# A two-layer hybrid decoder trunk: narrower gate maxima, paired transposes and another TensorE planner

## The chip, the cores and the metric

The kernel runs on one core of a Trainium2 chip. A core has several engines that work side by side, each through its own queue in order: TensorE (matmuls and transposes, called PE in the profile), VectorE (DVE), ScalarE (ACT), GpSimd (POOL) and SyncE (SP, which issues the DMAs here). The metric is the time of one execution in device microseconds, as the median of several runs. The profile's span runs from the first to the last instruction and is a little shorter than that time.

## The reference, cut to what matters

Two layers, sequence 256, model width 1024. Each layer normalises x, multiplies it by one wide input matrix, feeds three groups of heads, joins their outputs and adds the output projection to x. A last RMSNorm ends it.

```python
def hybrid_layer(x, norm_w, w_in, conv_w, conv_b, gate_bias, ret_norm_w, mlstm_norm_w, w_out):
    h = rmsnorm(x, norm_w)
    proj = jnp.matmul(h, w_in).astype(jnp.float32)
    (aq, ak, av, ag, bq, bk, bv, bg, cq, ck, cv, co, cg, ci, cf) = jnp.split(proj, cuts, axis=-1)
    # group A, 8 heads x 64: causal softmax attention with ALiBi, SiLU gate ag
    ya = merge_heads(moba_attention(...)) * jax.nn.silu(ag)
    # group B, 4 heads x 64: retention with fixed decays, head norm, SiLU gate bg
    yb = head_norm(retention(...), ret_norm_w) * jax.nn.silu(bg)
    # group C, 4 heads x 64: mLSTM on convolved q, k; gates i, f; output gate co; head norm; SiLU gate cg
    yc = head_norm(mlstm(...) * jax.nn.sigmoid(co), mlstm_norm_w) * jax.nn.silu(cg)
    y = jnp.concatenate([ya, yb, yc], axis=-1)
    return x + jnp.matmul(y, w_out)
```

With a sequence of 256 group A has one block, so it is plain causal attention. In group C each position's weights are exp of (a gate term of the key minus a running maximum of the gate terms up to the query). That running maximum, per head, is the "gate maxima" of the change:

```python
        d_log = jnp.where(causal, bt[..., :, None] - bt[..., None, :] + it[..., None, :], -jnp.inf)
        m_t = jnp.maximum(inter_log, jnp.max(d_log, axis=-1))
        w_intra = jnp.exp(d_log - m_t[..., None])
```

## The kernel before

All of x stays on the chip, transposed (features on partitions). Every fp32 operand of a projection is split into a high part in the rounded fp32r format and the rest (`hi`, `lo` for weights, `xx` for x, `yh`, `yl` for the gated outputs); ScalarE makes the high part, VectorE subtracts (`splitter`, `split_x`). A product is three TensorE matmuls, hi*hi, hi*lo and lo*hi, or one matmul of 512 columns for the first two and one of 256. Weights stream from HBM in chunks of about 1 MB into three buffers (`raw`).

The order of the work is not written by hand. Each piece of work is a Python generator (a "thread") that yields one operation at a time with an engine and an assumed cost in nanoseconds. `Sched.run` replays the threads in planned time. Each time it issues the operation that can start first on its engine; among equals the smaller priority number wins, then age. A result made on one engine counts as ready for another after `LAT` = 230 ns. What comes out is a fixed order of instructions for each engine; on the chip, semaphores make each instruction wait for its inputs, and each engine takes its instructions strictly in this order.

- `project` (priority 5) is the TensorE thread of the projections. It is almost always ready and fills what others leave.
- Small threads turn a projection's result into heads. Four PSUM banks `pj` hold projection results, four banks `mx` everything else.
- `head_a` does one head of group A: four score matmuls (`dots`) into an `mx` bank, VectorE's add of the ALiBi distances with a row maximum (`tensor_tensor_reduce`, "CUSTOM_DVE_ANT_0 sb<-mx,tb" in the profile), two exponentials on ScalarE into `sb`, three TensorE transposes of `sb` (128x128 each) into another `mx` bank, a ScalarE copy to `et`. `pair_a` starts two heads, waits for both, and multiplies with the values.
- Before its transposes `head_a` waits 400 ns of planned time more, by a `pause`; `norm` waits 500 ns between GpSimd's power (-0.5) and two transposes. These are the only two pauses.
- In group C, `evac_cv` computes the running maxima of 4 heads in `cu`, [4, 256], and copies columns 128 to 256 again behind them, so `cu` has 384. `ub` holds their high and low parts. `head_c` spreads one head's row to all 128 partitions by a matmul with a selecting matrix `sel` (384 columns, "mx<-ub,sel"); VectorE adds the causal mask, 384 columns of a table: keys 0 to 127 against all 256 queries, then keys 128 to 255 against queries 128 to 255.
- `y_out` transposes gated outputs for the output projection; `last_in`, `last_add`, `last_norm`, `last_out` are the end of the kernel.

The assumed TensorE costs stand in `M` and `TR`. Lines 259, 265, 280, 285, 288 and 494 or 1101 of the profile are the helpers that issue VectorE, ScalarE, matmul, transpose, DMA and GpSimd operations.

Of the kernel before, what the change touches and what calls it, by code (L numbers as in the profile page):

```python
# [110 lines left out]
class Sched:  # L111
# [2 lines left out]


    LAT = 230.0
    SELF = {"pe": 0.0, "dve": 130.0, "act": 130.0, "pool": 130.0, "sp": 0.0}

    def __init__(self):
# [68 lines left out]
    def run(self):  # L188
        while self.live:
            best = None  # L190
            for th in self.live:
                alt = None
                for way in th.req[1:]:
                    eng, cost, fn, after = way
                    if after is not None:
                        ready = after
                    elif th.src is None:
                        ready = th.t
                    else:
                        ready = th.t + (self.SELF[eng] if th.src == eng else self.LAT)  # L200
                    if after is None:
                        ready = max(ready, th.floor)
                    start = max(self.free.get(eng, 0.0), ready)
                    if alt is None or start + cost < alt[0]:
                        alt = (start + cost, start, way)
                prio = th.prio() if callable(th.prio) else th.prio
                key = (alt[1], prio, th.seq)
                if best is None or key < best[0]:
                    best = (key, th, alt[2])
            (start, _, _), th, (eng, cost, fn, after) = best  # L210
            self.live.remove(th)
            ins = fn()
            if self.log is not None:
                self.log.append((eng, start, start + cost, ins.ins.name))
            end = start + cost
            self.free[eng] = end
            th.t, th.src = end, eng
            self.step(th, end + self.LAT)

# [9 lines left out]
def trunk(ctx: ExitStack, tc: tile.TileContext, xp: bass.AP, w: bass.AP, fn: bass.AP,  # L229
# [7 lines left out]
    def sb_tile(shape, name, dt=F32):  # L237
        return cp.tile(shape, dt, name=name)
# [35 lines left out]
    def M(out, a, b, start, stop, after=None):  # L274
        n = _n(b)
        if a.dtype == F32R:
            cost = max(107.0, n / 2.4) + 3
        else:
            cost = 2 * max(107.0, n * 2 / 2.4 / 1.0) + 3
        return op("pe", cost, lambda: nc.tensor.matmul(out, a, b, start=start, stop=stop, skip_group_check=True),  # L280
                  after)

# [7 lines left out]
    def wait(ev):  # L290
        return ("wait", ev)
# [4 lines left out]
    def acq(tag):  # L296
        return ("acq", tag)

    def pause(t):

        ev = Event()
        ev.time = t
        return wait(ev)


    px = sb_tile([128, P_N + KT * S], "px")
    pr = px[:, :P_N]
# [12 lines left out]
    yh = sb_tile([128, KT, S], "yh", F32R)  # L320
    yl = sb_tile([128, KT, S], "yl", F32R)
    sel = sb_tile([128, 4, 128], "sel", F32R)
    ub = sb_tile([128, 384], "ub", F32R)
    cu = sb_tile([4, 384], "cu")
    gi = sb_tile([4, 2, S], "gi")
    on_a = sb_tile([128, 2, 512], "on_a")
    on_b = sb_tile([128, 2, 256], "on_b")
# [145 lines left out]
    def norm(l):  # L473

        ss = None
        for k in range(0, KT, 2):
            for z in (k, k + 1):
                yield wait(E("x0", z) if l == 0 else E("res", l - 1, z))
            sq = yield acq("t512")
            yield A(sq, x[:, k:k + 2, :].rearrange("p a t -> p (a t)"), AF.Square)  # L480
            if ss is None:
                ss = sq
            else:
                e = yield V("tensor_tensor", ss, ss, sq, op=OP.add)
                sc.release("t512", sq, e)
        yield V("tensor_tensor", ss[:, :256], ss[:, :256], ss[:, 256:], op=OP.add)
        p = yield acq("mx")
        for b in range(2):
            e = yield M(p[:, b:b + 1], ss[:, b * 128:(b + 1) * 128], ones[:, 0:1], b == 0, True)
        sc.release("t512", ss, e)  # L490
        ms = tiny(2)
        yield V("tensor_scalar", ms, p[:, 0:2], 1.0 / D_, EPS, op0=OP.mult, op1=OP.add)
        rs = tiny(2)
        e = yield G(630, lambda: nc.gpsimd.tensor_tensor(rs, ms, mhalf[:, :2], op=OP.pow))
        yield wait(E("tab"))
        yield pause(e + 500)
        for b in range(2):
            yield TR(p[:, 128 + b * 128:256 + b * 128], rs[:, b:b + 1].to_broadcast([128, 128]))
        rh = tiny(2)
        yield V("tensor_scalar", rh, rs, 0.5, None, op0=OP.mult)  # L500
        e = yield A(rrow, p[:, 128:384], AF.Copy)
        sc.release("mx", p, e)
        norms[l] = (rs, rh)
        sc.set(E("rs", l), e)
        yield prio(2)
        yield V("tensor_tensor", cr, tb[:, T_COS:T_COS + S], rrow, op=OP.mult)
        e = yield V("tensor_tensor", sr, tb[:, T_SIN:T_SIN + S], rrow, op=OP.mult)
        sc.set(E("cs", l), e)
# [318 lines left out]
    def pair_a(l, g, u, box):  # L827
        rs, rh = norms[l]
        et = yield acq("et")
        done = [Event(), Event()]  # L830
        for hh in range(2):
            sc.spawn(head_a(l, g, u, hh, et, done[hh]), 2)
        yield wait(done[0])
        yield wait(done[1])
        box[0] += 1
        if box[0] == 2:
            drop(l, (f"aq{g}", f"ak{g}"), done[1].time)
        yield wait(E("va", l))
        po = yield acq("mx")
        pv = po[:, :260].rearrange("p (b h e) -> p b h e", b=2, h=2)  # L840
        for hh in range(2):
            h = 4 * g + 2 * u + hh
            yield M(pv[:, 0, hh, :], et[:, hh, 0:128], va[:, 0, h, :], True, True)
            yield M(pv[:, 1, hh, :], et[:, hh, 128:256], va[:, 0, h, :], True, False)
            e = yield M(pv[:, 1, hh, :], et[:, hh, 256:384], va[:, 1, h, :], False, True)
        sc.release("et", et, e)
        rv = tiny(2, 2)
        yield V("reciprocal", rv, pv[:, :, :, HD])
        yield V("tensor_tensor", rv, rv, rh.unsqueeze(2).to_broadcast([128, 2, 2]), op=OP.mult)
        c0 = (4 * g + 2 * u) * HD  # L850
        e = yield V("tensor_tensor", on_a[:, :, c0:c0 + 128].rearrange("p b (h e) -> p b h e", e=HD),
                    pv[:, :, :, 0:HD], rv.unsqueeze(3).to_broadcast([128, 2, 2, HD]), op=OP.mult)
        sc.release("mx", po, e)
        sc.set(E("ona", l, 2 * g + u), e)

    def head_a(l, g, u, hh, et, done):
        h = 4 * g + 2 * u + hh
        s_ = yield acq("mx")
        yield from dots(s_, bufs[l, f"aq{g}"], bufs[l, f"ak{g}"], u, hh, QK_CUTS)
        sb = yield acq("sb")  # L860
        yield wait(E("tab"))
        m = tiny(2)
        f = 0.125 * 2.0 ** -(h + 1)
        for j, c in enumerate((slice(0, 128), slice(128, 384))):
            e = yield V("tensor_tensor_reduce", sb[:, c], s_[:, c], tb[:, T_DIST:T_DIST + 384][:, c], scale=1.0,
                        scalar=-3e38, op0=OP.add, op1=OP.max, accum_out=m[:, j:j + 1])
        sc.release("mx", s_, e)
        yield V("tensor_scalar", m, m, -f, None, op0=OP.mult)
        yield A(sb[:, 0:128], sb[:, 0:128], AF.Exp, scale=f, bias=m[:, 0:1])
        e = yield A(sb[:, 128:384], sb[:, 128:384], AF.Exp, scale=f, bias=m[:, 1:2])  # L870
        pt = yield acq("mx")
        yield pause(e + 400)
        for j in range(3):
            e = yield TR(pt[:, j * 128:(j + 1) * 128], sb[:, j * 128:(j + 1) * 128])
        sc.release("sb", sb, e)
        e = yield A(et[:, hh, :], pt[:, :384], AF.Copy)
        sc.release("mx", pt, e)
        sc.set(done, e)

    def evac_cqk(l, name, p, tag="pj"):  # L880
        t = 0 if name == "cq" else 2
# [22 lines left out]
    def evac_cv(l, name, ps):  # L904
# [32 lines left out]
        cb, ca = gi[:, 1], gi[:, 0]  # L937
        yield V("tensor_tensor_scan", cb, ones[0:4, 0:1].to_broadcast([4, S]), gi[:, 1], 0.0, op0=OP.mult, op1=OP.add)
        yield V("tensor_tensor", ca, gi[:, 0], cb, op=OP.subtract)
        yield V("tensor_tensor_scan", cu[:, :S], ca, ca, 0.0, op0=OP.max, op1=OP.max)  # L940
        yield V("tensor_copy", cu[:, S:], cu[:, 128:S], fast=True)
        yield V("tensor_copy", ub[0:4, :], cu, fast=True)
        e = yield V("tensor_tensor", ub[32:36, :], cu, ub[0:4, :].bitcast(F32), op=OP.subtract)
        sc.set(E("ub", l), e)
        yield V("tensor_tensor", cb, cb, cu[:, :S], op=OP.add)
        pm = yield acq("mx")
        pq = pm[:, :16].rearrange("p (a b h) -> p a b h", a=2, b=2)
        for a, src in ((0, ca), (1, cb)):
# [44 lines left out]
    def head_c(l, u, hh, et, done):  # L993
# [1 line left out]
        at = norms["at", l]  # L995
        yield wait(E("sel"))
        pu = yield acq("mx")
        yield M(pu[:, :384], sel[:, h, :], ub, True, True)
        wt = yield acq("sb")
        e = yield V("tensor_tensor", wt, pu[:, :384], tb[:, T_MC:T_MC + 384], op=OP.add)  # L1000
        sc.release("mx", pu, e)
        yield A(wt[:, 0:256], wt[:, 0:256], AF.Exp, scale=-1.0, bias=at[:, 0, 0, h:h + 1])
        e = yield A(wt[:, 256:384], wt[:, 256:384], AF.Exp, scale=-1.0, bias=at[:, 0, 1, h:h + 1])
# [157 lines left out]
    def consts():  # L1161
# [1 line left out]
        g = [128, 4, 128]  # L1163
        yield V("tensor_tensor", sel, ident[:, 0:4].unsqueeze(2).to_broadcast(g),
                ident[:, 32:36].unsqueeze(2).to_broadcast(g), op=OP.add)
        e = yield A(ub, tb[:, T_MC:T_MC + 384], AF.Copy, scale=0.0)
        sc.set(E("sel"), e)

    sc.spawn(loader(), 0)
# [41 lines left out]
```

## Time and profile before

| | |
|---|---|
| median of 3 runs | 301.76 us (301.43 to 303.13) |
| profiled execution | 301.41 us |
| its span | 299.6 us |
| mean granted TensorE clock | 0.995 |
| TensorE busy | 291.0 us, 97% |
| VectorE busy | 257.7 us, 86% |
| ScalarE busy | 196.6 us, 66% |
| GpSimd busy | 15.3 us, 5% |

In rows of groups, an operation is written as line, engine, operation, output<-inputs, shapes, count. In rows in order of time the first number is the start in us from the span's start, the second the time covered by the instructions merged in the row, x the count of them, and a bracket at the end gives the engine's idle time before the row and what ended it. Matmuls are pipelined, so durations of neighbours overlap.

### The profile page before, as it was taken

Reading aid. Unit: us, or ns where it says so; the run is one execution under the profiler, and the core shown is the slowest. Engines: PE = TensorE matmul, PEld = TensorE weight load, DVE = VectorE, ACT = ScalarE, POOL = GpSimd, SP = SyncE. Lnnn points to the kernel's source line nnn. Section 1 sums busy time; section 2 is a strip of 40 time slices with the busy share of each in tenths; the row PEclk is TensorE's granted clock in tenths of the full one; section 3 lists DMA queues with packets and bytes.
Section 4 is the critical chain, followed back from the end, with each engine's and each line's share of the span. In section 5 each row is a group of like instructions: output and inputs, shape, how many; then the busy total and the mean of one; then the engine's idle time right before and its main releaser. Section 6 shows DMA issues by size and latency. Waiting matters only on the chain.

```text
span 299.6 us, 4795 instructions
## 1 busy us (share of the span) xinstructions
PE 291.0 (97%) x1792; PEld 258.2 (86%) x1792; DVE 257.7 (86%) x549; ACT 196.6 (66%) x341; POOL 15.3 (5%) x19
## 2 busy tenths in 40 slices
PE   8899999999999999999999999999999999999991
PEld 6798989888989888899988898988899988888881
DVE  3969999999999997985679999999999999956353
ACT  5958997889448539644666699779555265845332
POOL 6000000000002002000020000000002002000010
PEclk9999999999999999999999999999999999999997
DMA  6999456574710560754317663446541624330003
GB/s 200 374 398 352 153 174 223 184 258 143 238 45 0 161 240 22 249 174 148 136 19 264 205 222 125 156 142 219 203 142 45 237 67 173 123 131 0 2 0 140
DMA packets 9095, 48.58 MB, mean 162 GB/s; under 512 B 1008, under 2 KB 1904, under 8 KB 4080
## 3 DMA queue, kind: packets, MB, share of 16 engines
q1 hardware_dynamic: 9072, 48.28, 46.7%
q8 instruction: 14, 0.23, 0.3%
q14 instruction: 9, 0.07, 0.1%
HBM read 47.23 MB, written 1.05 MB: 161 GB/s over the span
## 4 chain that ended last, share of the span: by engine, by line
PE 91%; DVE 2%; issue 2%; ACT 1%; DMA 1%; SPq 1%; POOL 0%; POOLq 0%
PE pj L280 71%; PE mx L280 15%; PE mx L285 4%; DMA px<-xp 1%; SPq L288 1%; DVE sb L259 1%; DVE t L259 1%; ACT t L265 0%; ACT hi L265 0%; POOL small L554 0%; ACT xx L265 0%; ACT raw L265 0%; POOLq L1207 0%; DVE raw L259 0%; DVE hc L259 0%
## 5 line engine op out<-in xcount | busy, mean ns | idle before, releaser
L259 DVE TENSOR_TENSOR lo<-raw,hi 128x1024 fp32r<-128x1024 f32 (+2 forms) x96 | 102.8, 1087 | 8.9 <-ACT hi L265 8.7
L265 ACT ACTIVATE hi<-raw 128x1024 fp32r<-128x1024 f32 (+2 forms) x96 | 88.8, 946 | 10.4 <-DMA raw<-w 4.6
L280 PE MATMUL pj<-hi,xx 128*128 128x512 f32 (+1 forms) x320 | 94.4, 374 | 0.0
L280 PE MATMUL pj<-xx,hi 128*128 128x512 f32 (+1 forms) x272 | 88.0, 377 | 0.7 <-ACT hi L265 0.7
L280 PE MATMUL pj<-xx,lo 128*128 128x256 f32 x240 | 68.8, 287 | 0.3 <-DVE lo L259 0.3
L280 PEld LDWEIGHTS pj<-hi,xx 128*128 128x128 f32 x320 | 57.4, 188 | 9.0
L280 PE MATMUL pj<-lo,xx 128*128 128x512 f32 (+1 forms) x160 | 59.4, 371 | 0.0
L280 PEld LDWEIGHTS pj<-xx,hi 128*128 128x128 f32 x272 | 49.9, 192 | 10.1 <-ACT hi L265 1.7
L280 PEld LDWEIGHTS pj<-xx,lo 128*128 128x128 f32 x240 | 45.8, 191 | 0.8 <-DVE lo L259 0.7
L280 PEld LDWEIGHTS pj<-lo,xx 128*128 128x128 f32 x160 | 30.1, 188 | 4.5
L265 ACT ACTIVATE sb<-sb,small 128x128 f32<-128x128 f32 (+1 forms) x48 | 19.5, 448 | 4.9 <-DVE small L259 2.4
L265 ACT ACTIVATE t<-pj 128x256 f32<-128x256 f32 x26 | 9.8, 376 | 17.0 <-PE pj L280 16.9
L265 ACT ACTIVATE st<-t 64x512 fp32r<-64x512 f32 x26 | 16.1, 627 | 4.5 <-DVE t L259 4.2
L1101 POOL TENSOR_TENSOR small<-small,mhalf 128x8 f32<-128x8 f32 x4 | 6.9, 1731 | 181.7 <-DVE small L259 181.7
L280 PE MATMUL pj<-yh,lo 128*128 128x256 f32 x56 | 15.9, 284 | 0.0
L280 PE MATMUL pj<-yh,hi 128*128 128x256 f32 x56 | 15.9, 284 | 0.0
L280 PE MATMUL pj<-yl,hi 128*128 128x256 f32 x56 | 15.8, 283 | 0.0
L280 PE MATMUL mx<-st,st 128*128 128x128 f32 (+1 forms) x64 | 15.1, 270 | 0.0
L265 ACT ACTIVATE t<-pj,small 128x512 f32<-128x512 f32 (+1 forms) x12 | 7.3, 610 | 11.2 <-PE pj L280 11.2
L259 DVE TENSOR_TENSOR t<-pj,t 128x256 f32<-128x256 f32 x26 | 10.9, 419 | 2.2 <-ACT t L265 2.1
L265 ACT ACTIVATE t<-t 32x512 f32<-32x512 f32 (+1 forms) x20 | 12.6, 629 | 0.3
L280 PEld LDWEIGHTS mx<-st,st 128*128 128x128 f32 x64 | 12.1, 189 | 0.6
(150 smaller groups left out, 480.3 us busy)
## 6 DMA issues: line engine op xcount, KB each, us to landing
raw<-w SPq DMA_DIRECT2D x37, 1024.0 KB, 4.8
raw<-w SPq DMA_DIRECT2D x2, 1056.0 KB, 6.2
raw<-w SPq DMA_DIRECT2D x6, 256.0 KB, 5.6
raw<-w SPq DMA_DIRECT2D x2, 512.0 KB, 6.8
tb<-tab SPq DMA_DIRECT2D x1, 960.0 KB, 10.0
px<-xp SPq DMA_DIRECT2D x3, 256.0 KB, 4.8
tb<-tab SPq DMA_DIRECT2D x1, 514.0 KB, 7.7
raw<-w SPq DMA_DIRECT2D x4, 128.0 KB, 2.8
```

The lines of the kernel that those rows point to most:

```text
L259: return op("dve", cost, lambda: getattr(nc.vector, name)(out, *a, **k), after)
L265: return op("act", cost, lambda: nc.scalar.activation(out, in_, func, **k), after)
L280: return op("pe", cost, lambda: nc.tensor.matmul(out, a, b, start=start, stop=stop, skip_group_check=True), after)
L285: return op("pe", 110.0, lambda: nc.tensor.transpose(out, in_, idn))
L288: return op("sp", cost, lambda: nc.sync.dma_start(out, in_))
L1101: yield G(1600, lambda: nc.gpsimd.tensor_tensor(vs, vs, mhalf[:, :8], op=OP.pow))
```

## The change

Three things change.

1. `cu` and `ub` have 256 columns; the copy of columns 128 to 256 is dropped. The matmul with `sel` has 256 columns. The mask is added in two VectorE operations, 256 and 128 columns, that both read the same bank.
2. `head_a` ends after its exponentials. `pair_a` waits for both heads, acquires two `mx` banks, does the six transposes one behind the other, then the two ScalarE copies.
3. The planner assumes longer TensorE distances, and orders TensorE differently: an operation whose input comes from another engine, or that had to wait for an event or a bank, is sorted as if ready `SLACK` = 400 ns later (its start in the plan is not moved). The two pauses are gone.

```diff
+    SLACK = 400.0
...
-                    start = max(self.free.get(eng, 0.0), ready)
+                    free = self.free.get(eng, 0.0)
+                    start = max(free, ready)
+                    by = max(free, ready + self.SLACK) if eng == "pe" and (th.src != "pe" or th.floor > th.t) else start
                     if alt is None or start + cost < alt[0]:
-                        alt = (start + cost, start, way)
+                        alt = (start + cost, start, way, by)
...
-                key = (alt[1], prio, th.seq)
+                key = (alt[3], prio, th.seq)
...
         if a.dtype == F32R:
-            cost = max(107.0, n / 2.4) + 3
+            cost = max(113.0, n / 2.4 + 13.5)
         else:
-            cost = 2 * max(107.0, n * 2 / 2.4 / 1.0) + 3
+            cost = 2 * max(108.0, n * 2 / 2.4 + 13.5)
...
         e = yield G(630, lambda: nc.gpsimd.tensor_tensor(rs, ms, mhalf[:, :2], op=OP.pow))
         yield wait(E("tab"))
-        yield pause(e + 500)
...
         for hh in range(2):
-            sc.spawn(head_a(l, g, u, hh, et, done[hh]), 2)
+            sc.spawn(head_a(l, g, u, hh, sbs, done[hh]), 2)
         yield wait(done[0])
         yield wait(done[1])
...
+        pts = []
+        for hh in range(2):
+            pt = yield acq("mx")
+            pts.append(pt)
+        for hh in range(2):
+            for j in range(3):
+                e = yield TR(pts[hh][:, j * 128:(j + 1) * 128], sbs[hh][:, j * 128:(j + 1) * 128])
+            sc.release("sb", sbs[hh], e)
+        for hh in range(2):
+            e = yield A(et[:, hh, :], pts[hh][:, :384], AF.Copy)
+            sc.release("mx", pts[hh], e)
...
         e = yield A(sb[:, 128:384], sb[:, 128:384], AF.Exp, scale=f, bias=m[:, 1:2])
-        pt = yield acq("mx")
-        yield pause(e + 400)
-        for j in range(3):
-            e = yield TR(pt[:, j * 128:(j + 1) * 128], sb[:, j * 128:(j + 1) * 128])
-        sc.release("sb", sb, e)
-        e = yield A(et[:, hh, :], pt[:, :384], AF.Copy)
-        sc.release("mx", pt, e)
-        sc.set(done, e)
+        sbs[hh] = sb
+        sc.set(done, e + Sched.LAT)
...
-        yield V("tensor_tensor_scan", cu[:, :S], ca, ca, 0.0, op0=OP.max, op1=OP.max)
-        yield V("tensor_copy", cu[:, S:], cu[:, 128:S], fast=True)
+        yield V("tensor_tensor_scan", cu, ca, ca, 0.0, op0=OP.max, op1=OP.max)
...
-        yield M(pu[:, :384], sel[:, h, :], ub, True, True)
+        yield M(pu[:, :S], sel[:, h, :], ub, True, True)
         wt = yield acq("sb")
-        e = yield V("tensor_tensor", wt, pu[:, :384], tb[:, T_MC:T_MC + 384], op=OP.add)
+        yield V("tensor_tensor", wt[:, :S], pu[:, :S], tb[:, T_MC:T_MC + S], op=OP.add)
+        e = yield V("tensor_tensor", wt[:, S:], pu[:, 128:S], tb[:, T_MC + S:T_MC + 384], op=OP.add)
```

An operation yields the planned end plus `LAT` as its value `e`, so an event set at `e + Sched.LAT` lies 460 ns of planned time behind the exponential's end.

More of the change, by code (lines that the diff above doesn't have):

```diff
@@ L202, in run @@
                         ready = max(ready, th.floor)
-                    start = max(self.free.get(eng, 0.0), ready)
+                    free = self.free.get(eng, 0.0)
+                    start = max(free, ready)
+                    by = max(free, ready + self.SLACK) if eng == "pe" and (th.src != "pe" or th.floor > th.t) else start
                     if alt is None or start + cost < alt[0]:
-                        alt = (start + cost, start, way)
+                        alt = (start + cost, start, way, by)
                 prio = th.prio() if callable(th.prio) else th.prio
-                key = (alt[1], prio, th.seq)
+                key = (alt[3], prio, th.seq)
                 if best is None or key < best[0]:
-                    best = (key, th, alt[2])
-            (start, _, _), th, (eng, cost, fn, after) = best
+                    best = (key, th, alt[2], alt[1])
+            _, th, (eng, cost, fn, after), start = best
             self.live.remove(th)
@@ L297, in acq @@
         return ("acq", tag)
[L299 to L303, printed above, removed]
     px = sb_tile([128, P_N + KT * S], "px")
@@ L322, in trunk @@
     sel = sb_tile([128, 4, 128], "sel", F32R)
-    ub = sb_tile([128, 384], "ub", F32R)
-    cu = sb_tile([4, 384], "cu")
+    ub = sb_tile([128, S], "ub", F32R)
+    cu = sb_tile([4, S], "cu")
     gi = sb_tile([4, 2, S], "gi")
@@ L830, in pair_a @@
         done = [Event(), Event()]
+        sbs = [None, None]
         for hh in range(2):
-            sc.spawn(head_a(l, g, u, hh, et, done[hh]), 2)
+            sc.spawn(head_a(l, g, u, hh, sbs, done[hh]), 2)
         yield wait(done[0])
@@ L854, in pair_a, with head_a @@
         sc.set(E("ona", l, 2 * g + u), e)
-    def head_a(l, g, u, hh, et, done):
+    def head_a(l, g, u, hh, sbs, done):
         h = 4 * g + 2 * u + hh
@@ L944, in evac_cv @@
         sc.set(E("ub", l), e)
-        yield V("tensor_tensor", cb, cb, cu[:, :S], op=OP.add)
+        yield V("tensor_tensor", cb, cb, cu, op=OP.add)
         pm = yield acq("mx")
@@ L1165, in consts @@
                 ident[:, 32:36].unsqueeze(2).to_broadcast(g), op=OP.add)
-        e = yield A(ub, tb[:, T_MC:T_MC + 384], AF.Copy, scale=0.0)
+        e = yield A(ub, tb[:, T_MC:T_MC + S], AF.Copy, scale=0.0)
         sc.set(E("sel"), e)
```

## The prediction, made before the result was known

> **What bounds the kernel now.** I read the span and the busy shares first, then the busy times by stretch, then what TensorE waited for (total, times, longest), and last its instructions in order of time.
>
> ```profile
> span 299.6 us, 4795 instructions
> PE 291.0 (97%) x1792; PEld 258.2 (86%) x1792; DVE 257.7 (86%) x549; ACT 196.6 (66%) x341; POOL 15.3 (5%) x19
> ```
>
> ```profile
> core 0: us, PE busy (x) PEld busy (x) DVE busy (x) ACT busy (x) POOL busy (x), PEclk, DMA share, GB/s
> 0.00:11.00 11.00, 8.59 (x37) 6.51 (x38) 5.80 (x17) 7.81 (x19) 4.50 (x11) 1.00 0.78 242
> 11.00:251.00 240.00, 240.00 (x1507) 214.81 (x1507) 222.34 (x462) 164.92 (x278) 9.24 (x6) 1.00 0.51 176
> 251.00:257.00 6.00, 5.82 (x37) 4.91 (x36) 5.93 (x28) 4.58 (x10) 0.00 (x0) 1.00 0.50 176
> 257.00:288.00 31.00, 31.00 (x183) 27.08 (x181) 18.07 (x33) 15.27 (x29) 0.00 (x0) 1.00 0.16 52
> 288.00:299.60 11.60, 5.55 (x36) 4.89 (x34) 5.55 (x13) 4.00 (x10) 1.59 (x2) 0.86 0.24 90
> ```
>
> ```profile
> PE mx L372 <- DVE sb L370: 1.4, 1, 1.4
> PE pj L280 <- ACT hi L265: 0.7, 1, 0.7
> PE pj L280 <- DVE lo L259: 0.3, 1, 0.3
> PE mx L285 <- DVE t L259: 0.2, 1, 0.2
> ```
>
> From 11 us to 288 us TensorE is never out of work except for 0.2 us in the stretch 251 to 257; the other three waits lie in the first 11 us, where the loads and their splitting set the pace. So there are only two ways to change the time: give TensorE less to issue, or make it wait. A busy matmul row overlaps its neighbour, so below I price TensorE by the distance from one start to the next, not by duration. VectorE is the next engine: 222.3 of 240 us busy in the long stretch, 5.93 of 6 where TensorE's one wait lies.
>
> **The change part by part.** *Gate maxima over 256 columns.* Eight matmuls (four heads, two layers) stream 256 columns in place of 384.
>
> ```profile
> 87.55 0.69 PE L280 MATMUL mx<-ub,sel 128*128 128x384 f32 x3
> 88.08 0.40 PE L280 MATMUL pj<-xx,hi 128*128 128x512 f32 x1
> ```
>
> ```profile
> 88.55 0.28 PE L280 MATMUL pj<-xx,lo 128*128 128x256 f32 x1
> 88.67 0.40 PE L280 MATMUL pj<-xx,hi 128*128 128x512 f32 x1
> ```
>
> Three of 384 columns take 88.08 - 87.55 = 0.53 us, 0.177 each; one of 256 takes 0.12. 8 x 0.057 = 0.45 us less, all of it on the path, since nothing runs beside TensorE that sets the end.
>
> VectorE pays for it: the biased copy of 384 columns becomes one of 256 and one of 128.
>
> ```profile
> 88.13 0.41 DVE L259 TENSOR_TENSOR t<-pj,t 128x256 f32<-128x256 f32 x1
> 88.46 1.01 DVE L259 TENSOR_TENSOR sb<-mx,tb 128x384 f32<-128x384 f32 x2
> 89.39 0.41 DVE L259 TENSOR_TENSOR t<-pj,t 128x256 f32<-128x256 f32 x1
> ```
>
> ```profile
> 37.16 0.29 DVE L259 CUSTOM_DVE_ANT_0 sb<-mx,tb 128x128 f32<-128x128 f32 x1
> 37.37 0.09 DVE L259 DVE_READ_ACCUMULATOR2_ANT small<- 128x1 f32 x1
> ```
>
> ```profile
> 186.03 0.41 DVE L259 CUSTOM_DVE_ANT_0 sb<-mx,tb 128x256 f32<-128x256 f32 x1
> 186.37 0.08 DVE L259 DVE_READ_ACCUMULATOR2_ANT small<- 128x1 f32 x1
> ```
>
> The two of 384 take 89.39 - 88.46 = 0.93, 0.465 each; a 256 from a PSUM bank takes 0.33 (88.13 to 88.46); the nearest row of 128 columns is the other kind of VectorE operation that reads PSUM, 0.21. So 0.54 against 0.465: +0.075 x 8 = 0.6 us of VectorE. The copy that widened the maxima goes, once a layer, and two small operations a layer and one ScalarE fill shrink from 384 to 256 columns. I take VectorE's balance as nothing: it is hidden under the 17.7 us that VectorE has idle between 11 and 251. Were that cover gone, 0.6 us would be the price. [...]
>
> *Six transposes in one run.* A pair now fetches two banks after both heads' exponentials, does 2 x 3 transposes and then both copies. Sixteen runs of three become eight of six.
>
> ```profile
> 57.46 0.49 PE L285 MATMUL mx<-tb,sb 128*128 128x128 f32 x3
> 57.71 0.48 PE L280 MATMUL pj<-hi,xx 128*128 128x512 f32 x1
> 58.02 0.40 PE L280 MATMUL pj<-lo,xx 128*128 128x512 f32 x1
> ```
>
> ```profile
> 256.11 0.27 PE L285 MATMUL mx<-tb,t 128*128 128x128 f32 x1
> 256.56 0.55 PE L285 MATMUL mx<-tb,t 128*128 128x128 f32 x3 [0.18 <-DVE t L259]
> 256.95 0.82 PE L285 MATMUL mx<-tb,sb 128*128 128x128 f32 x6
> 257.52 0.48 PE L280 MATMUL pj<-lo,xx 128*128 128x512 f32 x1
> 257.83 0.49 PE L285 MATMUL mx<-tb,sb 128*128 128x128 f32 x3
> ```
>
> A run of three costs 0.25 us to the next matmul, whose own distance is then 0.31 in place of some 0.23 for 512 columns (the 355 ns a pair below, less 0.12): 0.33 in all. One run of six already happens, from 256.95: 0.57 + 0.08 = 0.65 against 2 x 0.33. That is 0.01 to 0.02 for a pair, 7 pairs, 0.1 us. Each transpose costs 0.11 wherever it stands. [...]
>
> What the run may cost: the first head's bank is asked for later and two are held at once, out of four. TensorE works in order, so if the second exponential is late, six transposes and every projection matmul queued behind them wait; the value matmuls and the outputs of the pair come later by one head. That is off the path:
>
> ```profile
> 265.71 0.42 DVE L259 TENSOR_TENSOR on_a<-mx,small 128x256 f32<-128x256 f32 x1
> ```
>
> ```profile
> 272.67 1.43 DVE L259 TENSOR_TENSOR t<-t,on_a 128x256 f32<-128x256 f32 x4
> ```
>
> the last attention output is finished at 266.1 and first used at 272.7.
>
> *The plan's TensorE distances, its slack, the pauses dropped.* No instruction is added; the order on all engines is planned anew. The old costs are columns/2.4 + 3 ns, 216.3 + 109.7 = 326 ns for a matmul of 512 and one of 256; the new ones give 226.8 + 120.2 = 347. Eight such pairs stand between these two rows:
>
> ```profile
> 40.14 0.28 PE L280 MATMUL pj<-xx,lo 128*128 128x256 f32 x1
> ```
>
> ```profile
> 42.98 0.28 PE L280 MATMUL pj<-xx,lo 128*128 128x256 f32 x1
> ```
>
> 2.84 us, 355 ns a pair. So the real TensorE came 8% later than planned, which gave every helper an unplanned lead; now it is 2%. What the lead is worth:
>
> ```profile
> 42.74 0.51 ACT L265 ACTIVATE sb<-sb,small 128x256 f32<-128x256 f32 x1
> ```
>
> ```profile
> 43.32 0.49 PE L285 MATMUL mx<-tb,sb 128*128 128x128 f32 x3
> ```
>
> ```profile
> 55.26 1.19 ACT L265 ACTIVATE sb<-sb,small 128x256 f32<-128x256 f32 x3
> ```
>
> ```profile
> 154.60 1.60 POOL L494 TENSOR_TENSOR small<-small,mhalf 128x2 f32<-128x2 f32 x1 [38.46 <-DVE small L259]
> ```
>
> ```profile
> 156.58 0.38 PE L285 MATMUL mx<-tb,small 128*128 128x128 f32 x2
> ```
>
> The first transposes start 43.32 - 43.25 = 0.07 us after their exponential: next to no lead. The third run had 57.46 - 56.45 = 1.0. Over the roughly 8 us from a head's scores to its transposes the lost 6% is 0.5 us; in exchange the planned distance grows from 230 + 400 to 230 + 230 + 400 ns (the pair's event adds one latency). Net -0.27, so a site with 0.07 waits 0.2 us, one with 1.0 not at all. I take the first sort for two of eight pairs, rounded up to 0.3 us. Layer 2's norm: its POOL power took 1.60 us against the 0.63 planned and ended 0.38 before the transposes; their planned distance falls from 730 to 630 ns and the drift goes too. Another 0.2 us. All other helpers (gate outputs, value matmuls) had no slack in the plan and now have 400 ns, so TensorE's wait at 256.11 (0.45 us to the next transpose where 0.11 is usual) should go: -0.34.
>
> Bounds of new waits: none at all, or all that the plan still under-costs on VectorE. Its reduce over the scores is planned at columns/1.3, 98 and 197 ns; the rows above say 210 and 340. That is 0.25 us a head, 16 heads, 4.1 us. I take 0.5, near the low end, because the rows of the old plan with the same fault show one wait only. Loads, SP's queue and POOL's small operations are not moved past anything new; the first 11 us and the tail after 288 leave the plan no choice on TensorE.
>
> Sum, against the profiled execution's own 301.41 us (span 299.6 and 1.8 around it): 301.41 - 0.45 - 0.1 - 0.34 + 0.5 = 301.0. That execution lies at the fast end of the runs shown (median 301.76, lowest 301.43), so the median may sit 0.3 above the sum.
>
> **The rivals.** *Slower: the drift was the margin.* With TensorE planned truly and VectorE still planned too fast, the pair's second exponential comes late. For it: VectorE's 222.3 of 240 us, and that the only late wait is on VectorE. Against it: 17.7 us of idle time that lets it catch up, and the new 860 ns. It decides once VectorE is behind by more than 0.86 us at the pairs; at 0.4 us a pair, three quarters of the 4.1 us, the time is 301.0 - 0.5 + 3.1 = 303.6.
>
> *Faster: the switch costs more than I read.* The 0.08 us after each run may be a toll for changing between transposes and projections; eight runs fewer then save 0.7, and if no new wait comes, 301.41 - 0.45 - 0.34 - 0.7 = 299.9. Against it: the matmul after a run of three starts 57.71 - (57.46 + 2 x 0.11) = 0.03 us behind the last transpose, 0.08 sooner than a transpose would, which pays the 0.08 back; and the run of six at 256.95.
>
> *Nothing moves.* The new order leaves its own waits of a microsecond and spends the 0.9 us gained: 301.4 to 301.8. For it: 277 us of TensorE work that no order can shorten.
>
> **How the numbers follow.** A measurement here tells about 0.5%, 1.5 us, from no change. My sum has 0.47, around 300.3 to 301.9; nothing moves 0.22; the slower rival 0.18, of which I leave the upper half out of the range; the faster one 0.13, mostly beyond 0.5% because the median before lies at 301.76, its lower half left out. That gives same 0.69, slower 0.18, faster 0.13, and 299.7 to 303.5 for 8 in 10.
>
> **What the profile after would show.** The gate matmuls start 0.12 apart, not 0.177. Transposes on the exponentials come as x6. TensorE still fills 11 to 288 us, ending some 0.4 us earlier; the wait near 256 is gone; small new ones stand at pair transposes (on ScalarE's exponential) and at layer 2's norm (on POOL). TensorE waits of over 2.4 us in all, on exponentials or on split weights, would make the forecast wrong on the slow side; projection distances under 0.35 a pair, or fewer idle microseconds before 11 us, on the fast side.

## The result and the profile after

The changed kernel takes 305.89 us (median of 4, 305.52 to 307.35) against 301.6 beside it (4 runs, 300.63 to 303.13): a ratio of 1.0146, 95% interval 1.0125 to 1.0167. It is slower by 4.3 us, where 301.0 was predicted and 303.5 was the upper end. The profile below is of the execution at 307.35 us (span 305.6), whose TensorE was granted a clock of 0.50 from 11.7 to 15.1 us (mean granted clock of the execution 0.988; the other three have 0.996 to 0.998 and spans of 303.7 to 304.3), which cost it some 1.5 us that their spans leave no room for; so I compare the stretches from 15 us on.

The span and the busy shares of the changed kernel, from its page:

```profile
span 305.6 us, 4795 instructions
PE 294.3 (96%) x1792; PEld 259.3 (85%) x1792; DVE 258.4 (85%) x554; ACT 197.2 (65%) x342; POOL 17.6 (6%) x19
```

As many matmuls as before, 6 us more of span, and VectorE and ScalarE less than 1 us busier. No engine got work that would explain the time. The next two rows are the shares of each engine in the chain that ended last, before and then after:

```profile
PE 91%; DVE 2%; issue 2%; ACT 1%; DMA 1%; SPq 1%; POOL 0%; POOLq 0%
```

```profile
PE 46%; DVE 36%; ACT 8%; issue 5%; DMA 2%; POOL 1%; SPq 1%; POOLq 0%; DVEq 0%; ACTq 0%
```

Before, the chain back from the end stayed on TensorE for 91%. After, it leaves TensorE at a wait and then follows VectorE for long stretches. One wait late in the kernel is enough to turn it off TensorE, so the shares say where to look and not how much was lost. The waits say that. TensorE's waits in the changed kernel (total, times, longest):

```profile
PE mx L370 <- DVE sb L368: 1.4, 1, 1.4
PE mx L289 <- DVE small L263: 1.1, 1, 1.1
PE pj L284 <- ACT hi L269: 1.1, 2, 0.9
PE mx L284 <- ACT va L269: 0.4, 1, 0.4
PE mx L289 <- ACT et L269: 0.3, 1, 0.3
PE pj L284 <- DVE lo L263: 0.3, 1, 0.3
PE mx L289 <- ACT sb L269: 0.3, 1, 0.3
PE mx L284 <- DVE et L263: 0.2, 1, 0.2
PE mx L284 <- DVE hc L263: 0.2, 1, 0.2
```

The first, the third and the sixth lie before 15 us, as before. The other six, 2.5 us, are new, and each is for another operation. Three are for a result that TensorE reads: gate values (`small`), values (`va`) and exponentials (`sb`). The other three, `et` by ScalarE, `et` by VectorE and a group C output (`hc`), are not read by the TensorE operation that waits; what makes them empties an `mx` bank, so there TensorE waits for the bank. Measured by the distances from start to start, as the prediction prices TensorE, I count 4.1 us above the usual distances at nine places, 0.18 to 1.25 each, because a short wait hides in part under the modelled end of the matmul before it. The longest of them, with the rows ahead of it:

```profile
214.77 0.28 PE L284 MATMUL mx<-st,st 128*128 128x256 f32 x1
214.89 0.38 PE L289 MATMUL mx<-tb,small 128*4 128x128 f32 x2
216.36 0.38 PE L289 MATMUL mx<-tb,small 128*4 128x128 f32 x2 [1.09 <-DVE small L263]
```

The same four transposes of layer 2's gate values before the change:

```profile
213.82 0.60 PE L285 MATMUL mx<-tb,small 128*4 128x128 f32 x4
```

They stood in one run; now the second two start 1.47 us after the first two, and everything queued on TensorE stands behind them. Where the lost time lies, by stretch, before (columns as in the prediction):

```profile
15.00:115.00 100.00, 100.00 (x608) 88.54 (x607) 94.81 (x206) 72.46 (x121) 2.85 (x3) 1.00 0.55 194
115.00:140.00 25.00, 25.00 (x189) 23.64 (x188) 19.12 (x35) 15.61 (x25) 1.14 (x1) 1.00 0.51 169
140.00:286.00 146.00, 145.81 (x889) 128.92 (x888) 127.64 (x268) 91.98 (x155) 5.24 (x3) 1.00 0.39 134
```

and after:

```profile
11.00:15.00 4.00, 3.84 (x20) 3.84 (x21) 4.00 (x13) 4.00 (x13) 0.00 (x0) 0.59 1.04 411
15.00:115.00 100.00, 99.29 (x605) 87.62 (x605) 92.60 (x199) 69.89 (x115) 3.21 (x2) 1.00 0.55 195
115.00:140.00 25.00, 25.00 (x176) 23.01 (x175) 20.83 (x46) 16.88 (x30) 1.64 (x1) 1.00 0.40 130
140.00:286.00 146.00, 144.16 (x885) 127.00 (x884) 128.48 (x270) 93.56 (x157) 6.69 (x3) 1.00 0.41 141
```

The 2.5 us that TensorE is short of work are spread over both long stretches; 115 to 140 us, the end of layer 1, is full. Keep that middle row in mind: five of the experiments lose time there.

The parts that the prediction priced by rows came as priced. A gate maxima matmul and a joined run of transposes in the changed kernel:

```profile
92.69 0.64 PE L284 MATMUL mx<-ub,sel 128*128 128x256 f32 x4
93.16 0.40 PE L284 MATMUL pj<-xx,hi 128*128 128x512 f32 x1
...
117.27 0.81 PE L289 MATMUL mx<-tb,sb 128*128 128x128 f32 x6
117.84 0.47 PE L284 MATMUL pj<-hi,xx 128*128 128x512 f32 x1
```

Four of 256 columns take 0.47 us, 0.12 each, and a run of six takes 0.57.

### The profile page after: what moved, and what is told of

Its sections match the earlier page's. It is cut to its first block, busy times and chain, and to the rows that moved or that the text cites. A ratio compares the mean times of both kernels' runs of the same rounds, so it can differ in the third digit from the quotient of the medians.

```text
span 305.6 us, 4795 instructions
## 1 busy us (share of the span) xinstructions
PE 294.3 (96%) x1792; PEld 259.3 (85%) x1792; DVE 258.4 (85%) x554; ACT 197.2 (65%) x342; POOL 17.6 (6%) x19
## 4 chain that ended last, share of the span: by engine, by line
PE 46%; DVE 36%; ACT 8%; issue 5%; DMA 2%; POOL 1%; SPq 1%; POOLq 0%; DVEq 0%; ACTq 0%
PE pj L284 34%; DVE lo L263 11%; PE mx L284 10%; DVE t L263 8%; DVE st L263 4%; PE mx L289 3%; DVE small L263 3%; DVE sb L263 3%; ACT hi L269 3%; ACT t L269 3%; DMA raw<-w 2%; DVE zd L263 1%; DVE et L263 1%; DVE hc L263 1%; SPq L292 1%
## 5 line engine op out<-in xcount | busy, mean ns | idle before, releaser
L284 PE MATMUL pj<-xx,lo 128*128 128x256 f32 x240 | 69.7, 290 | 0.3 <-DVE lo L263 0.3
L284 PEld LDWEIGHTS pj<-xx,hi 128*128 128x128 f32 x272 | 50.7, 196 | 10.4 <-ACT hi L269 2.2
L269 ACT ACTIVATE st<-t 64x512 fp32r<-64x512 f32 x28 | 17.4, 628 | 4.7 <-DVE t L263 3.9
L1104 POOL TENSOR_TENSOR small<-small,mhalf 128x8 f32<-128x8 f32 x4 | 8.4, 2093 | 183.6 <-DVE small L263 183.6
L284 PEld LDWEIGHTS mx<-va,et 128*128 128x128 f32 x96 | 11.6, 191 | 1.0 <-ACT va L269 0.7
L284 PE MATMUL mx<-va,et 128*128 128x65 f32 x96 | 11.6, 273 | 0.4 <-ACT va L269 0.4
```

What stands on the lines that cost most here:

```text
L269: return op("act", cost, lambda: nc.scalar.activation(out, in_, func, **k), after)
L1104: yield G(1600, lambda: nc.gpsimd.tensor_tensor(vs, vs, mhalf[:, :8], op=OP.pow))
```

## The experiments

Three theories went in. **The lost lead (theory 1):** the old plan had TensorE 8% too fast, and the lead that this gave the helpers covered costs that the plan has too low on VectorE and ScalarE; with true TensorE distances those late results show, at many places. **The sort rule (theory 2):** with its slack it hands work to the helpers too late. **The joining (theory 3):** it makes a pair wait for its later head. e2 and e3 came out against the last two, and e1 showed something that none of the three had; from e5 on the rival of theory 1 is **the new order:** any re-planning puts the work in another order, and the old order was a lucky one. Another rival came up on the way: that a wait which is mended only shows the next one.

In every table row the ratio is against the kernel before on the same chip. The last two columns are TensorE's waits by the profile, us: at the end of layer 1 (115 to 140 us), and in the rest from 15 to 288. They are added up from rounded rows, so they hold to 0.1 us, and they are of one execution each.

| kernel | median us | ratio (95%) | 115–140 | rest |
|---|---|---|---|---|
| before | 301.6 | | 0 | 0.2 |
| after | 305.89 | 1.0146 (1.0125–1.0167) | 0 | 2.5 |
| e1 old distances | 311.35 | 1.0324 (1.0282–1.0366) | 3.7 | 0 |
| e2 no slack | 306.94 | 1.0183 (1.0140–1.0225) | 0 | 5.0 |
| e3 no joining | 305.98 | 1.0137 (1.0109–1.0165) | 0 | 3.0 |
| e4 new distances alone | 307.86 | 1.0194 (1.0167–1.0221) | 0.3 | 3.3 |
| e5 gates alone | 306.62 | 1.0172 (1.0142–1.0202) | 2.2 | 0 |
| e6 slack 800 | 304.75 | 1.0102 (1.0080–1.0123) | 0 | 2.2 |
| e7 joining alone | 302.82 | 1.0044 (1.0026–1.0062) | 0 | 0.5 |
| e8 slack alone | 303.94 | 1.0083 (1.0063–1.0103) | 1.0 | 0.8 |
| e9 gates, order frozen | 301.18 | 0.9993 (0.9969–1.0017) | 0 | 0.4 |
| e10 VectorE plus 1 ns | 303.95 | 1.0081 (1.0049–1.0112) | 1.0 | 0 |
| e11 distances part way | 303.94 | 1.0089 (1.0055–1.0122) | 0 | 1.3 |
| e12 slack 800, gates later | 303.93 | 1.0078 (1.0052–1.0103) | 0 | 1.1 |
| e13 true helper costs | 305.51 | 1.0136 (1.0097–1.0175) | 2.3 | 0 |
| e14 true costs, C first | 300.84 | 0.9967 (0.9950–0.9985) | 0 | 0 |
| e15 C first alone | 305.89 | 1.0132 (1.0101–1.0162) | 0.3 | 2.6 |
| e16 gates alone, C first | 301.78 | 1.0004 (0.9988–1.0019) | 0 | 0 |

**e1, the change with the old distances.**

```diff
-            cost = max(113.0, n / 2.4 + 13.5)
+            cost = max(107.0, n / 2.4) + 3
...
-            cost = 2 * max(108.0, n * 2 / 2.4 + 13.5)
+            cost = 2 * max(107.0, n * 2 / 2.4 / 1.0) + 3
```

> The changed kernel with the old assumed TensorE distances (columns/2.4 + 3 ns); everything else of the change stays. Theory 1, the lost lead (the plan's too fast TensorE was an unplanned margin that covered VectorE's and ScalarE's too cheap costs): most of the 4.3 us comes back, 301 to 302.5 us, TensorE waits after 15 us under 1 us. Theory 2 (the new sort rule with SLACK hands work to the helpers too late) and theory 3 (joined transposes make a pair wait for its later head) both say no better: 305 to 306.

It came out 5.5 us slower than the change itself. Theory 1 was right that the spread waits go (none outside 115 to 140 us) and wrong about the time, since something it had no place for appeared. Its row for the end of layer 1:

```profile
115.00:140.00 25.00, 21.21 (x111) 18.26 (x111) 21.05 (x68) 10.69 (x24) 2.54 (x1) 0.73 0.30 109
```

111 matmuls where the old kernel does 189, at a granted clock of 0.73: a hole. Its waits are for exponentials of group A (3.3 of 3.7 us, the longest 2.1). So there are two mechanisms, the spread waits and this hole.

**e2, without the slack, with the old pauses.**

```diff
-                    by = max(free, ready + self.SLACK) if eng == "pe" and (th.src != "pe" or th.floor > th.t) else start
+                    by = start
...
+        yield pause(e + 500)
...
-        sc.set(done, e + Sched.LAT)
+        sc.set(done, e + 400)
```

> The changed kernel sorted by planned start as before (no SLACK), with the two pauses of 400 and 500 ns back; new distances and joined transposes stay. Theory 1: no better, 305 to 307 us, since the gates' and value matmuls lose their 400 ns too. Theory 2: back to 301 to 302. Theory 3: 305 to 306.

Theory 2 is out: without its sort rule the kernel is no faster. The waits double, as the lost lead has it: the slack gives back part of what the distances take. How much that is in time is not clear, since the intervals of e2 and of the change overlap, and e2's trace is of an execution of 309.08 us, 2 us above its median.

**e3, each head does its own transposes and its copy.**

```diff
-        sbs[hh] = sb
-        sc.set(done, e + Sched.LAT)
+        pt = yield acq("mx")
+        for j in range(3):
+            e = yield TR(pt[:, j * 128:(j + 1) * 128], sb[:, j * 128:(j + 1) * 128])
+        sc.release("sb", sb, e)
+        e = yield A(et[:, hh, :], pt[:, :384], AF.Copy)
+        sc.release("mx", pt, e)
+        sc.set(done, e)
```

> The changed kernel with each head's three transposes and copy done by the head itself, as before; new distances and SLACK stay. Theory 1 and 2: 305 to 306 us. Theory 3: 301 to 302.

305.98 against 305.89: theory 3 is out. e3 has another order too, so what can be told is that joining together with the order it brings changes nothing, in either direction.

**e4, the kernel before with the new distances and nothing else.**

```diff
-            cost = max(107.0, n / 2.4) + 3
+            cost = max(113.0, n / 2.4 + 13.5)
...
-            cost = 2 * max(107.0, n * 2 / 2.4 / 1.0) + 3
+            cost = 2 * max(108.0, n * 2 / 2.4 + 13.5)
```

> The kernel before with only the two cost lines of TensorE changed to the new distances. Theory 1: 304 to 306 us, with TensorE waits of 3 us or more after 15 us that the kernel before does not have. Theories 2 and 3: as before, 301 to 302.

Two numbers in the planner, no instruction changed, and 6.2 us more, beyond even what theory 1 gave. Its TensorE waits from 15 us on:

```profile
PE mx L285 <- ACT sb L265: 1.8, 4, 0.8
PE mx L285 <- DVE small L259: 0.6, 1, 0.6
PE mx L285 <- ACT et L265: 0.6, 2, 0.3
PE mx L280 <- DVE et L259: 0.4, 1, 0.4
PE mx L280 <- DVE on_b L259: 0.3, 1, 0.3
```

The same kind of waits as after the change, with exponentials foremost, whose planned distance to their transposes is 630 ns here and 860 after the change. With e1 this shows that the new distances bring the spread waits.

**e5, e7 and e8, one part of the change at a time on the kernel before.** e5 has the narrower gate maxima alone, e7 the joined transposes alone, e8 the new sorting rule without the pauses.

```diff
# e5
-        yield M(pu[:, :384], sel[:, h, :], ub, True, True)
+        yield M(pu[:, :S], sel[:, h, :], ub, True, True)
...
# e7
+        for hh in range(2):
+            for j in range(3):
+                e = yield TR(pts[hh][:, j * 128:(j + 1) * 128], sbs[hh][:, j * 128:(j + 1) * 128])
...
-        sc.set(done, e)
+        sc.set(done, e + 400)
...
# e8
-                key = (alt[1], prio, th.seq)
+                key = (alt[3], prio, th.seq)
```

> The kernel before with only the 256-column gate maxima; old distances, old sort rule, pauses. By the prediction's sum alone 301.4 - 0.45 = 301.0. Theory 1 (the planned TensorE distances make the loss) agrees: 300.8 to 301.7. Rival (any edit of a cost or an operation re-plans all engines, and the order found before cannot be kept; a hole as in the changed kernel with old distances, which stands at 120 to 136 us there, comes from this edit): 305 or more, with TensorE waits of some 3 us between 115 and 140.

> The kernel before with only the joined transposes (after both heads, 400 ns of planned pause kept). Theory 1: 301 to 302. Rival of the re-planned order: 305 or more if the hole at 120 to 136 us comes from this edit, else 301 to 302.5.

> The kernel before with only the new sort rule (SLACK 400, no pauses); old distances. Theory 1: 301 to 302. Rival of the re-planned order: 305 or more if the hole comes from the sort rule.

e7 costs 0.44%, where leaving the joining out gained nothing in e3. e5, which takes 0.45 us of work off TensorE, costs 1.7%, and e8 0.8%; both with a hole at 115 to 140 us (e5's TensorE is 22.77 of 25 us busy there). The lost lead has no room for that, since neither touches the distances. The new order has, though e7, at 302.82 us, and e8, at 303.94, fell between the forecasts of both.

**e6, twice the slack.**

```diff
-    SLACK = 400.0
+    SLACK = 800.0
```

> The changed kernel with SLACK 800 in place of 400: twice the planned distance between a helper's result and TensorE's use of it. Theory 1 in its plain form (helpers come late by up to 1.2 us, so a longer planned distance replaces the lost lead): TensorE waits after 15 us fall from some 4 us to under 2, time 302.5 to 304. Rival (the helpers are the bound there, so work handed on later comes out later and the waits only move): 305 to 307.

Better than the change by 0.4%, and between the two forecasts. What is left are the gate-value transposes of both layers (2.0 of 2.2 us).

**e9, the gate edit with the old plan.** The operations are the change's, the planned costs those of before, so every engine has the old order.

```diff
-        yield M(pu[:, :384], sel[:, h, :], ub, True, True)
+        yield op("pe", 384 / 2.4 + 3, lambda: nc.tensor.matmul(pu[:, :S], sel[:, h, :], ub, start=True, stop=True,
+                                                               skip_group_check=True))
...
+        e = yield op("dve", 384 / 0.96 + 69, mask)
```

> The kernel before with the 256-column gate maxima, but each edited step planned at its old cost (384 columns, the dropped copy kept as a placeholder in the plan), so that the planned order of every engine is the one before. Both theories that blame the order (lost lead; re-planned order): the edit by itself is worth 8 x 0.057 = 0.45 us, so 301.0, ratio 0.9985. If the edit itself costs (VectorE's split mask copies on the path): 302 to 303.

In the traces TensorE and ScalarE do the same operations in the same order as before, and VectorE's order differs at the edit alone. It is no slower, and by its median 0.3 us faster, inside the interval. The edit as such is harmless; all that e5 lost, it lost to the new order.

**e10, the kernel before with 1 ns more for each VectorE operation in the plan.**

```diff
-        cost = n / (1.92 if fast else 0.96) + 69
+        cost = n / (1.92 if fast else 0.96) + 70
```

> The kernel before with one number changed: VectorE's assumed fixed cost 70 ns in place of 69. No instruction changes. Theory 1 (lost lead of TensorE's planned distances): 301 to 302, the drift is untouched. Rival (the order before stands at an edge; any re-planning can let group C's helpers fall behind the weight splits and leave TensorE without work at the end of layer 1): 303 to 305, with TensorE idle between 115 and 135 us and none elsewhere.

2.5 us slower, by a number that no instruction sees. VectorE's rows of the last group C output `hc` in layer 1 and of the first low part `yl` for the output projection, before:

```profile
117.39 0.69 DVE L259 TENSOR_TENSOR hc<-hc,small 128x512 f32<-128x512 f32 x1
...
122.15 0.48 DVE L259 SCALAR_TENSOR_TENSOR yl<-mx,px,yh 128x256 fp32r<-128x256 f32 x1
```

and in e10:

```profile
123.47 0.69 DVE L259 TENSOR_TENSOR hc<-hc,small 128x512 f32<-128x512 f32 x1
...
126.86 0.47 DVE L259 SCALAR_TENSOR_TENSOR yl<-mx,px,yh 128x256 fp32r<-128x256 f32 x1
```

Group C ends 6 us later. TensorE has no projection left by then and waits for the gated outputs; its rows in e10:

```profile
127.38 0.39 PE L280 MATMUL pj<-yl,hi 128*128 128x256 f32 x1 [0.27 <-DVE yl L259]
128.62 0.38 PE L280 MATMUL pj<-yh,hi 128*128 128x256 f32 x1 [0.38 <-ACT yh L265]
129.37 0.38 PE L280 MATMUL pj<-yl,hi 128*128 128x256 f32 x1 [0.37 <-DVE yl L259]
```

That is the hole: the old order had group C through VectorE just in time, and nothing in the planner keeps it there. The traces of all the kernels agree: in the five with a hole (e1, e5, e8, e10, e13) this last `hc` of layer 1 starts at 121.7 us or later, in all others at 119.7 or sooner.

**e11, distances part way, +7 ns for +3.**

```diff
-            cost = max(107.0, n / 2.4) + 3
+            cost = max(107.0, n / 2.4) + 7
```

> The kernel before with TensorE's assumed cost 4 ns higher (columns/2.4 + 7 and 111 least), some 40% of the way to the new distances. Theory 1: waits spread over the kernel, a part of those with the new distances alone (which took 6.2 us): 302.5 to 304.5, at the transposes of exponentials and of small gate values. Rival (only a hole at the end of layer 1 costs, and the spread waits are chance): 301 to 302.

Nearly half of e4's loss (0.89 of 1.94%), with spread waits and no hole, the longest again at the gate values. The lost lead holds by degrees.

**e12, slack 800 and a pause of 1300 ns ahead of the gate-value transposes.**

```diff
-    SLACK = 400.0
+    SLACK = 800.0
...
+        yield pause(e + 1300)
```

> The changed kernel with SLACK 800 and 1300 ns more of planned time before the four transposes of the gate values, where the kernel with SLACK 800 still waited 1.1 and 1.2 us. Theory 1: those two waits go too, 302 to 303. Rival (the waits only move to the next step of group C): 304 to 305.

By the medians 0.2% better than e6, with intervals that overlap, and between the two forecasts. The gate-value waits are gone, and half of what they took is back at other places (0.8 us for group B's outputs). The rival that waits move on holds in part: mending sites one at a time does not end.

**e13, true helper costs in the changed kernel.** The score reduce measures 210 and 343 ns from start to start for 128 and 256 columns, planned 98 and 197. Operations on 64 or 32 partitions come late about half of the time: of those that start back to back with the next in the changed kernel's trace, 12 of 26 on VectorE (64 partitions) take 88 to 102 ns more than planned from start to start and the rest at most 10, and 10 of 16 on ScalarE take 116 to 142 more and the rest 13 to 32. On VectorE the traces show where: `zd`, on partitions 64 to 127, takes 702 or 703 ns in this trace and in that of before, where 602 is planned, and `zu`, on partitions 0 to 63, takes 598 to 610 unless `zd` comes next (690 to 698). By these rows the 0.1 us goes with a step from one half of the partitions to the other. One row of the changed kernel, three of ScalarE on 64 partitions:

```profile
29.84 1.90 ACT L269 ACTIVATE st<-t 64x512 fp32r<-64x512 f32 x3
```

633 ns each, planned 507. The edit, which charges 110 ns for every such operation and so rather too much than too little:

```diff
-            cost = n / 1.3
+            cost = n / 0.96 + 77
...
+        if out.shape[0] == 64:
+            cost += 110
...
+        if out.shape[0] in (32, 64):
+            cost += 110
```

> The changed kernel with VectorE's and ScalarE's planned costs set to the distances in the traces: the score reduce columns/0.96 + 77 in place of columns/1.3, and 110 ns more for operations on 32 or 64 partitions. Theory 1 (spread waits come from helpers planned too cheap): TensorE has no idle time from 15 to 115 and from 140 to 286 us (less than 0.5 us in all), and, since VectorE is now planned fuller, the hole at 115 to 140 opens, 3 to 4 us: 304 to 305.5. Rival (the spread waits are chance of the order): they stay, 1.5 us or more outside 115 to 140.

Exactly the lost lead's pattern: with the same new distances the spread waits are gone, every one. Which of the two corrections does it was not tried. The time stays, since the new order has the hole. e13 by stretch:

```profile
15.00:115.00 100.00, 100.00 (x605) 88.46 (x604) 93.65 (x196) 72.45 (x118) 2.85 (x2) 1.00 0.55 193
115.00:140.00 25.00, 22.66 (x157) 20.98 (x156) 19.57 (x48) 14.18 (x27) 2.54 (x1) 0.93 0.38 127
140.00:286.00 146.00, 146.00 (x906) 130.16 (x905) 127.81 (x267) 95.28 (x160) 4.88 (x3) 1.00 0.42 141
```

**e14, e13 with group C first; e15 and e16, its controls.** e14 is e13 and this; e15 is the changed kernel and this; e16 is e5 and this.

```diff
-            sc.spawn(pair_c(l, u, box), 2, e2)
+            sc.spawn(pair_c(l, u, box), 0, e2)
...
-            sc.spawn(head_c(l, u, hh, et, done[hh]), 2)
+            sc.spawn(head_c(l, u, hh, et, done[hh]), 0)
```

> The same with group C's pairs and heads at priority 0 in place of 2, so that on VectorE they go ahead of weight splits and group A that could start at the same moment. Both theories together (helper costs make the spread waits, group C's lateness makes the hole): neither is left, 300 to 301.5, not slower than the kernel before. If another cause stands behind the hole: 303 or more.

> The changed kernel with group C at priority 0 alone; helper costs as the change has them. Theory 1: the spread waits stay, 303 to 306. Rival (group C's order was all): 300 to 302.

> The kernel before with the 256-column gate maxima (which alone took 5.2 us more) and group C at priority 0; old distances. If group C's lateness opens the hole, it closes: 300.5 to 301.7, ratio 0.997 to 1.001. If not: 304 or more.

e14 by stretch:

```profile
15.00:115.00 100.00, 100.00 (x607) 88.57 (x606) 93.81 (x204) 73.93 (x122) 3.21 (x2) 1.00 0.55 194
115.00:140.00 25.00, 25.00 (x189) 23.67 (x188) 19.63 (x41) 15.27 (x27) 2.54 (x1) 1.00 0.50 168
140.00:286.00 146.00, 146.00 (x894) 129.57 (x893) 128.62 (x270) 93.12 (x158) 5.25 (x3) 1.00 0.39 134
```

TensorE is full in all three, and the time is 300.84 us over 12 runs, below both kernels. e15 keeps the spread waits and the time of the change: the priority alone does nothing for them. e16 closes e5's hole (25.00 of 25) and wins back 4.8 us: the priority alone is enough for the hole. So the corrected costs mend the spread waits and the priority mends the hole, each only its own. The table says the same of the spread waits over all orders: 0 to 0.8 us with the old distances, 1.3 part way, 1.1 to 5.0 with the new ones and the old helper costs, none with both corrected. The priority was tried on the holes of e5 and e13; that it would close e1's, whose waits are for group A's exponentials, is not shown.

## Why the prediction was wrong

**The step that failed is the term of +0.5 us for new waits.** The runs show 4.1 us in its place, by start distances, from 15 us on. I took the low end "because the rows of the old plan with the same fault show one wait only". That argument was circular: the old plan showed one wait because of the very lead that the change removes, so its rows could not bound the waits without it. The upper bound, also 4.1 us, was the better number, though that the two agree is chance: besides the score reduce about half of the operations on part of the partitions come late too, of 52 on VectorE by some 0.1 us and of 44 on ScalarE by 0.13, by my estimate about 6 us more, which I had not looked for. The 0.5 was also badly added up: two pairs at 0.2 us are 0.4 and not 0.3. Layer 2's norm, to which it gave the other 0.2, shows no wait.

**The slower rival had the right mechanism.** "The drift was the margin" is what e4, e11 and e13 show. Its place was too narrow, the pairs' exponentials: the slack covers most of those, and only 0.7 us by start distances stands there (0.26 at 63.5, 0.41 at 188.2), while gate values, values and the emptying of `mx` banks, to which I gave 400 ns and no further thought, have most of the rest. The mark that I set for being wrong on the slow side, 2.4 us of waits, was passed at other places than the two I named. Its 303.6 us fell 2.3 short. The 17.7 us of idle VectorE that I held against it were no protection: VectorE has 29 us idle between 15 and 286 us after the change too, and the waits stand there all the same.

**Costing the edits one by one was wrong in kind.** Each edit's own cost was near my figure: the gate maxima -0.45 us, 0.12 a matmul as priced, harmless with the order frozen (e9); the joining nothing that e3 can tell. But every edit has the planner order all engines anew, and that moved the time by up to 5 us (e5) and by 2.5 us for 1 ns (e10). I wrote "the order on all engines is planned anew" and priced it at nothing.

**The wait at 256.11** went from its place, but its 0.34 us was not saved; 0.18 and 0.43 us stand near it now, at 263.4 and 264.6. VectorE's extra mask operation stayed hidden, as said.

**Nothing moves** fell with the sum; **faster** too: the joined runs take 0.57 us, as priced, and show no toll for switching (nor would eight runs at 0.08 us have been 0.7, but 0.64). Whether the joining saves its 0.1 us the runs cannot tell (305.98 without it, 305.89 with it, in another order).

**The sum as it came out,** from the span before of 299.6: -0.45 for the gates, -0.53 for waits of before that left their places, +4.1 for new ones, +0.4 by which the changed kernel comes later out of its first 11 us (10.79 to 11.16 for the matmul that waits there for `lo`), 303.1. The profiled span less its 1.5 us of half clock, 304.1, and the spans of the other runs, 303.7 to 304.3, leave about 1 us that I have not placed. It has no one place: no other distance from 15 to 288 us is more than 0.13 us above the usual.

Three things stay open: why a step between the halves of the partitions takes some 0.1 us, whether ScalarE's late operations are of the same kind, and whether e14's gain over the kernel before, 0.33%, would survive the next edit, since its order comes from the same planner.

## What to carry to other kernels

Where a planner writes the order, its errors on different engines can cancel: correct the costs of all engines together, or a truer number for one can make the kernel slower. A missing wait in a trace does not bound what waits once the margin is gone; add up what the plan under-costs on the helpers instead. And to judge a small edit, freeze the order or try a 1 ns change first: a gap that moves by 2 us for 1 ns will swallow any saving, until the work that must not be late is given priority by name.

## What the hardware showed beside that

In e13's hole idle time on TensorE cost more than itself. TensorE waits 0.93 and 1.01 us there, and the matmuls behind the second one come at about half speed for 3 us:

```profile
127.06 0.39 PE L288 MATMUL pj<-yl,hi 128*128 128x256 f32 x1 [0.93 <-DVE yl L265]
...
129.06 0.58 PE L288 MATMUL pj<-yl,hi 128*128 128x256 f32 x1 [1.01 <-DVE yl L265]
129.44 0.41 PE L288 MATMUL pj<-yh,lo 128*128 128x256 f32 x1
129.65 0.41 PE L288 MATMUL pj<-yh,hi 128*128 128x256 f32 x1
...
131.99 0.28 PE L288 MATMUL pj<-yh,lo 128*128 128x256 f32 x1
132.10 0.28 PE L288 MATMUL pj<-yh,hi 128*128 128x256 f32 x1
```

0.21 us from start to start in place of 0.12, and from 129 to 132 us that is another 1.3 us lost behind waits that take 3.2 us by start distances; less the gates' 0.45 and the 0.53 of waits that the old order had, that is 3.5, against the 3.3 us by which its span, 302.9, is longer than before. The granted clock fell with it: 1.00 up to 128 us, a mean of 0.64 from 128 to 130 and of 0.51 from 130 to 132, and 1.00 again from there, which makes 3.4 us at 0.50. Its waits there, 0.39, 0.93 and 1.01 us, lie between 125.1 and 129.1 us.

Five kernels have waits of 1.0 us and more in all between 115 and 140 us. TensorE's idle time in those 25 us and its mean granted clock there are 3.79 us and 0.73 in e1, 2.34 and 0.93 in e13, 2.23 and 0.93 in e5, 1.14 and 1.00 in e8 and in e10. e5, with waits of 0.60, 0.56 and 1.03 us, has its matmuls 0.21 or 0.22 us apart from 131.12 to 132.19 us too; e8 and e10, with three waits each of 0.3 to 0.4, lost no clock. e1 does 78 matmuls fewer there than the kernel before, which at its 0.13 us a matmul (25 us, 189) is by my estimate 10 us, near the 9.9 us by which its span, 309.5, is longer and well above its idle time. The spread waits of the changed kernel, up to 1.1 us each and far apart, leave TensorE idle for 1.84 us from 140 to 286 us, and the clock there is 1.00. What decides when it falls is not shown.
